# A third extra seven-product unit in each half of a SwiGLU down product: units (9, 13, 19) and (5, 9, 13) instead of (9, 19) and (5, 13)

## The chip, the cores and the metric

The kernel runs on one core of a Trainium2 chip. The metric is the device time of one execution in microseconds (us), the median of several runs. The engines that matter here are TensorE (PE, matmuls), its weight loader (PEld), VectorE (DVE), ScalarE (ACT) and SyncE (SP), which issues the loads of weights. Each of them takes its instructions in the order of its own queue, and an instruction that waits holds up all that stand behind it.

## What is computed

One decoder layer on 256 tokens of width 2048: a SwiGLU feed-forward block (FFN), a mixer of two gated linear attentions, and a second FFN, each with a norm before and a norm after it. The change lies in the last matrix product of both FFNs, `hidden @ w_down`, with a hidden width of 5504.

```python
def swiglu(x, w_gate, w_up, w_down):
    return (jax.nn.silu(x @ w_gate) * (x @ w_up)) @ w_down

f1 = swiglu(rms_norm(h, ffn1_pre_norm[l]), ffn1_w_gate[l], ffn1_w_up[l], ffn1_w_down[l])
h = h + 0.5 * rms_norm(f1, ffn1_post_norm[l])
...
f2 = swiglu(rms_norm(h, ffn2_pre_norm[l]), ffn2_w_gate[l], ffn2_w_up[l], ffn2_w_down[l])
h = h + 0.5 * rms_norm(f2, ffn2_post_norm[l])
```

## The kernel before

All products are exact to float32 by splitting each operand into a high and a low part: ACT writes the high part (`whi`, L151), DVE the rest (`wlo`, L153), and `mm3` (L155 to L159) makes one product of a 128x128 block of activations and a 128x512 block of weights by three matmuls: high x high (L157), low activations x high weights (L158), high activations x low weights (L159).

`down_proj` (L587) makes the down product in two halves of 1024 output columns. A half has two column blocks of 512 (`i` = 0, 1), there are two blocks of 128 tokens (`t` = 0, 1), and the hidden width is cut into 43 k tiles of 128. The four sums of a half, c00, c01, c10 and c11, stay in PSUM. Two k tiles make a unit: units 0 to 20, and one single k tile (42). A plain unit takes 2 x 2 x 2 = 8 products, that is 24 matmuls, and its weights are two chunks of 128x1024, each split by one ACT and one DVE instruction.

A unit of the list `DSUMS + DMORE[hf]` is done by Strassen's scheme in the form of Winograd (`Blocks.seven`, L265): seven products, that is 21 matmuls, but sums of weight blocks have to be made first. DVE makes three adds (`wsum`, `raw`, `wsum`, L243), then the three low parts: two of 128x1024 (`wlo`, L243) and one of 128x1536 (`wsuml`, L243). ACT makes four high parts (L278, L280, L282, L284), and SP issues four loads of 256 KB (L272 to L275) where a plain unit has two of 512 KB. The seven products go to four shared sums (p1, p5, p6, p7) and three of the c; `share` (L304) and `close` (L317) add the p to the c at the end of the half.

A seven unit also needs sums of activation blocks. `sums_of(u)` (L756) makes them one unit ahead: four small DVE operations (L203 to L206), then ACT (high) and DVE (low). They are kept in `parts`, which both halves share, so a unit that is in both halves is summed once. Where they are kept differs: units 3, 7, 11 and 15 have homes of their own, and the units of `DMORE` take buffers from `new_part`:

```python
def new_part(i):
    s = ("hkhi", "hklo")[i]
    return fwork.tile([P, 2, NT * P], F32R, tag=s, name=nm(s), bufs=4)
```

There are four buffers of `hkhi` and four of `hklo`. The same buffers take the split activations of every unit (`get`, L739, through L151 and L153): one `hkhi` and one `hklo` for each unit, 22 times in each half. A buffer is free again when the last matmul that reads it is done. So sums of activations that lie in them take from the buffers in which the units' own activations are prepared ahead of PE. Before, unit 9's sums are held only until unit 9 of the first half is done, 19's likewise, and 5's and 13's in the second half.

The weights have rings of five buffers (`raw`, `whi`, `wlo`), so ACT and DVE can be about five chunks ahead of PE. The order of instructions on each engine is fixed when the program is built: a scheduler takes the instructions in the order of the code, and where a buffer is not free it lets other work of that engine go first. `weigh` (L600) squares a finished c on ACT (L452) and multiplies it with the post norm on DVE (L608).

Of the kernel before, what the change touches and what calls it, by code (L numbers as in the profile page):

```python
# [31 lines left out]
SUMS = (2, 4, 6)  # L32
FOUR = (2, 4, 5, 6)
DSUMS = (3, 7, 11, 15)
DMORE = ((9, 19), (5, 13))
DTAIL = 7
O_GQ, O_GK, O_GV, O_GO, O_CODE = 0, 512, 1024, 2048, 3072
O_HQ, O_HF, O_HI, O_HO, O_ZG, O_ZH = 3088, 4112, 5136, 6160, 7184, 9232
# [48 lines left out]
def kernel(ctx: ExitStack, tc: tile.TileContext, a: dict, out: bass.AP):  # L87
# [499 lines left out]
    def down_proj(w_dram, nkt, lhs, sums_of, post, pre, wpost, ys, homes, following):  # L587
# [30 lines left out]
        for hf in range(2):  # L618
# [4 lines left out]
            n = nkt - DTAIL if hf else nkt  # L623
            units = sorted(DSUMS + DMORE[hf])
            kt = 0
# [49 lines left out]
    def ffn(pre, x, rs, post, pre_next, begin=None, ready=(), then=None):  # L675
        with ExitStack() as fctx:
# [4 lines left out]
# [3 lines that stand above are left out]
# [72 lines left out]
            def sums_of(u):  # L756
# [3 lines left out]
                          *[f[:, k * P:(k + 1) * P] for k in range(4)])  # L760
                if any(u in more for more in DMORE):
                    hi, lo = [new_part(i).rearrange("p i c -> p (i c)") for i in range(2)]
# [600 lines left out]
```

## Time and profile before

| | |
|---|---|
| median of 3 runs | 2080.27 us (2080.07 to 2080.61) |
| the profiled execution | 2080.67 us |
| its span, first to last instruction | 2078.8 us |
| PE busy | 2067.8 us |
| DVE busy | 1854.7 us |
| ACT busy | 1239.7 us |
| down product of the first FFN | from about 466 to 692 us of the span |
| down product of the second FFN | from about 1844 to 2070 us |

Times in rows of the timeline are microseconds from the start of the span, then the duration, engine, line, operation, output, inputs and form. Where a row has brackets, they give the idle time of the engine before it and what ended it. Instructions overlap: an engine's next instruction can start before the one ahead has ended, so the step from start to start is what an engine needs for one. Of a matmul the end is modelled.

### The profile page before, as it was taken

The page shows a single profiled execution, that of the slowest core. Times are in us where ns is not written, and L with a number is a line of the kernel's source. Part 1 is how long each engine was busy: PE and PEld are TensorE (multiplying, and loading weights), DVE is VectorE, ACT ScalarE, POOL GpSimd, SP SyncE. Part 2 cuts the span into 40 slices and gives each one's busy share as a digit, 9 for nine tenths or more (in the row PEclk, how much of TensorE's full clock was granted, in tenths as well). Part 3 has the DMA queues.
Part 4 walks back from the last instruction along what each step waited for, and adds up shares of the span by engine and source line. Part 5 has one row for each costly group of instructions (what it writes and reads, how often), then busy time and mean ns, then how long its engine had stood idle before and what let it go on. Part 6 is the DMA issues. An engine that isn't in the chain of part 4 may idle for free.

```text
span 2078.8 us, 29319 instructions
## 1 busy us (share of the span) xinstructions
PE 2067.8 (99%) x10509; PEld 1721.1 (83%) x10509; DVE 1854.7 (89%) x2187; ACT 1239.7 (60%) x1670; POOL 40.6 (2%) x87
## 2 busy tenths in 40 slices
PE   9999999999999999999999999999999999999998
PEld 7888888898888888878888888888888888898886
DVE  7898999989999879989999897578999989999896
ACT  6555656565666576576655554465555655666663
POOL 1000000000000100000000000010000000000000
PEclk9999999999999999999999999999999999999999
DMA  8566656656667467555565666755666657576663
GB/s 267 183 210 199 211 188 194 214 183 226 208 195 233 153 192 232 163 168 188 174 203 186 184 221 214 220 179 172 222 200 186 209 186 224 165 239 201 198 208 132
DMA packets 200665, 412.23 MB, mean 198 GB/s; under 512 B 18036, under 2 KB 26423, under 8 KB 200520
## 3 DMA queue, kind: packets, MB, share of 16 engines
q1 hardware_dynamic: 194896, 401.80, 61.0%
q10 hardware_dynamic: 5624, 8.57, 1.3%
q8 instruction: 82, 1.34, 0.3%
q14 instruction: 63, 0.52, 0.1%
HBM read 406.11 MB, written 4.19 MB: 197 GB/s over the span
## 4 chain that ended last, share of the span: by engine, by line
PE 96%; ACT 1%; DVE 1%; issue 0%; DMA 0%; POOL 0%; SPq 0%; DVEq 0%; POOLq 0%; ACTq 0%
PE c L157 22%; PE c L159 21%; PE c L158 21%; PE p L159 5%; PE p L158 5%; PE p L157 5%; PE mm L157 3%; PE mm L159 3%; PE mm L158 3%; PE ps L397 2%; PE acc L157 1%; PE acc L158 1%; PE acc L159 1%; PE ps L905 0%; DVE h L510 0%
## 5 line engine op out<-in xcount | busy, mean ns | idle before, releaser
L151 ACT ACTIVATE whi<-raw 128x1024 fp32r<-128x1024 f32 (+3 forms) x498 | 510.6, 1033 | 279.8 <-PE c L158 114.7
L153 DVE TENSOR_TENSOR wlo<-raw,whi 128x1024 fp32r<-128x1024 f32 (+3 forms) x498 | 587.5, 1190 | 86.6 <-ACT whi L151 85.3
L157 PE MATMUL c<-whi,xhi 128*128 128x512 f32 (+1 forms) x1270 | 495.8, 391 | 0.5 <-DVE hq L849 0.3
L159 PE MATMUL c<-wlo,xhi 128*128 128x512 f32 (+1 forms) x1270 | 490.8, 387 | 0.0
L158 PE MATMUL c<-whi,xlo 128*128 128x512 f32 (+1 forms) x1270 | 490.5, 386 | 0.0
L243 DVE TENSOR_TENSOR wlo<-raw,whi 128x1024 fp32r<-128x1024 f32 (+1 forms) x252 | 294.5, 1203 | 11.9 <-ACT whi L278 6.3
L159 PEld LDWEIGHTS c<-wlo,xhi 128*128 128x128 f32 x1270 | 238.4, 188 | 47.2 <-DVE wlo L153 0.3
L157 PEld LDWEIGHTS c<-whi,xhi 128*128 128x128 f32 x1270 | 238.5, 188 | 46.9 <-issue 0.7
L158 PEld LDWEIGHTS c<-whi,xlo 128*128 128x128 f32 x1270 | 238.6, 188 | 44.9
L282 ACT ACTIVATE whi<-raw 128x1024 fp32r<-128x1024 f32 (+1 forms) x126 | 131.8, 1046 | 204.5 <-DVE raw L243 78.5
L243 DVE TENSOR_TENSOR wsuml<-wsum,wsumh 128x1536 fp32r<-128x1536 f32 (+1 forms) x126 | 218.0, 1730 | 33.7 <-ACT wsumh L284 33.6
L157 PE MATMUL c<-whi,hkhi 128*128 128x512 f32 x558 | 217.0, 389 | 0.0
L159 PE MATMUL c<-wlo,hkhi 128*128 128x512 f32 x558 | 216.8, 388 | 0.0
L158 PE MATMUL c<-whi,hklo 128*128 128x512 f32 x558 | 216.7, 388 | 0.0
L280 ACT ACTIVATE wsumh<-wsum 128x1024 fp32r<-128x1024 f32 (+1 forms) x126 | 131.5, 1044 | 108.6 <-DVE wsum L243 74.7
L278 ACT ACTIVATE whi<-raw 128x1024 fp32r<-128x1024 f32 (+1 forms) x126 | 131.4, 1043 | 100.2 <-PE c L158 84.7
L243 DVE TENSOR_TENSOR wsum<-raw,raw 128x1024 f32<-128x1024 f32 (+1 forms) x126 | 151.8, 1205 | 20.5 <-DMA raw<-in_ffn_w_down_dram 17.3
L159 PEld LDWEIGHTS c<-wlo,hkhi 128*128 128x128 f32 x558 | 104.8, 188 | 21.6
L158 PEld LDWEIGHTS c<-whi,hklo 128*128 128x128 f32 x558 | 104.8, 188 | 21.3
L157 PEld LDWEIGHTS c<-whi,hkhi 128*128 128x128 f32 x558 | 104.8, 188 | 21.3
L243 DVE TENSOR_TENSOR c<-c,psum 128x512 f32<-128x512 f32 (+1 forms) x135 | 86.6, 682 | 11.8 <-PE c L159 11.4
L243 DVE TENSOR_TENSOR wsum<-raw 128x512 f32<-128x512 f32 (+1 forms) x126 | 86.0, 683 | 3.6
(347 smaller groups left out, 3117.1 us busy)
## 6 DMA issues: line engine op xcount, KB each, us to landing
raw<-in_ffn_w_down_dram SPq DMA_DIRECT2D x124, 512.0 KB, 4.6
raw<-in_w_in_dram SPq DMA_DIRECT2D x104, 512.0 KB, 4.5
raw<-in_ffn_w_up_dram SPq DMA_DIRECT2D x97, 512.0 KB, 4.5
raw<-in_ffn_w_gate_dram SPq DMA_DIRECT2D x96, 512.0 KB, 4.7
raw<-in_ffn_w_gate_dram SPq DMA_DIRECT2D x128, 256.0 KB, 3.8
raw<-in_w_in_dram SPq DMA_DIRECT2D x128, 256.0 KB, 3.5
raw<-in_ffn_w_up_dram SPq DMA_DIRECT2D x126, 256.0 KB, 3.8
raw<-in_ffn_w_down_dram SPq DMA_DIRECT2D x96, 256.0 KB, 4.0
```

The lines of the kernel that those rows point to most:

```text
L151: last[0] = nc.scalar.activation(hi, src, AF.Copy)
L153: nc.vector.tensor_tensor(lo, src, hi.bitcast(F32), op=ALU.subtract)
L157: nc.tensor.matmul(ps, lhsT=xhi, rhs=whi, start=start, stop=False)
L158: nc.tensor.matmul(ps, lhsT=xlo, rhs=whi, start=False, stop=False)
L159: nc.tensor.matmul(ps, lhsT=xhi, rhs=wlo, start=False, stop=stop)
L243: return nc.vector.tensor_tensor(o, x, y, op=op)
L278: nc.scalar.activation(ahi, ra, AF.Copy)
L280: nc.scalar.activation(hi[:, 0:2, :], wsum[:, 0:2, :], AF.Copy)
L282: nc.scalar.activation(bhi, rb, AF.Copy)
L397: end = nc.tensor.transpose(dst_ps[:, i * P:(i + 1) * P], src[:, i * P:(i + 1) * P], ident)
```

## The change

One table is changed: which units beside 3, 7, 11 and 15 are done with seven products, in the first and in the second half of the down product. It holds for both FFNs.

```diff
-DMORE = ((9, 19), (5, 13))
+DMORE = ((9, 13, 19), (5, 9, 13))
```

Unit 13 of the first half and unit 9 of the second become seven units. Units 9 and 13 are now in both halves, so their sums are made in the first half and held until the second half has used them. PE has 12 matmuls fewer, DVE 16 instructions more, ACT 8 more, and SP issues 16 loads of 256 KB in place of 8 of 512 KB. The order of the work changes at three places, the same in both FFNs; the numbers below are of the first FFN.

The first place is DVE at the step from unit 11 to unit 12 of the first half. Before, `hklo_996` is the low part of unit 12's activations, and `wlo_994` and `wlo_999` are the low parts of unit 12's weights:

```order
L243 TENSOR_TENSOR wlo_987_4679<-raw_981_4669,whi_986_4678 128x1024
L153 TENSOR_TENSOR hklo_996_4724<-hT_563_2734,hkhi_995_4723 128x512
L243 TENSOR_TENSOR wlo_989_4681<-raw_982_4670,whi_988_4680 128x1024
L243 TENSOR_TENSOR wsuml_985_4673<-wsum_983_4671,wsumh_984_4672 128x1536
L153 TENSOR_TENSOR wlo_994_4720<-raw_992_4717,whi_993_4719 128x1024
L153 TENSOR_TENSOR wlo_999_4742<-raw_997_4739,whi_998_4741 128x1024
```

Now, at the same place on DVE, `sums_992` and `hklo_994` are the sums of unit 13, `wlo_997` and `wlo_1002` the weights of unit 12, and `hklo_999` is unit 12's activations:

```order
L243 TENSOR_TENSOR wsuml_985_4673<-wsum_983_4671,wsumh_984_4672 128x1536
L153 TENSOR_TENSOR wlo_997_4729<-raw_995_4726,whi_996_4728 128x1024
L203 TENSOR_TENSOR sums_992_4717<-hT_563_2734 128x128
L205 TENSOR_TENSOR sums_992_4717<-hT_563_2734 128x128
L204 SCALAR_TENSOR_TENSOR sums_992_4717<-sums_992_4717,hT_563_2734 128x128
L153 TENSOR_TENSOR wlo_1002_4751<-raw_1000_4748,whi_1001_4750 128x1024
L206 TENSOR_TENSOR sums_992_4717<-hT_563_2734,sums_992_4717 128x128
L153 TENSOR_TENSOR hklo_994_4723<-sums_992_4717,hkhi_993_4722 128x512
L153 TENSOR_TENSOR hklo_999_4733<-hT_563_2734,hkhi_998_4732 128x512
L243 TENSOR_TENSOR wsum_1005_4768<-raw_1003_4766,raw_1004_4767 128x1024
```

Unit 12's activations have moved from ahead of unit 11's last two low parts to behind unit 13's sums, and ACT's high part of them likewise.

The second place is the end of the first half. The rows are DVE before: `hklo_1102` is the activations of unit 0 of the second half, `psum` the shared sums, c00 to c11 the finished sums of the first half, and `y` their product with the post norm:

```order
L243 TENSOR_TENSOR psum_1074_5083<-psum_1074_5083,p7_909_4318 128x512
L153 TENSOR_TENSOR hklo_1102_5176<-hT_106_590,hkhi_1101_5175 128x512
L243 TENSOR_TENSOR psum_1075_5084<-psum_1074_5083,p5_908_4317 128x1024
L153 TENSOR_TENSOR hklo_1107_5210<-hT_106_590,hkhi_1106_5209 128x512
L153 TENSOR_TENSOR wlo_1105_5206<-raw_1103_5203,whi_1104_5205 128x1024
L243 TENSOR_TENSOR c00_865_4150<-c00_865_4150,psum_1074_5083 128x512
```

Now on DVE `hklo_1108` is the activations of that unit 0:

```order
L243 TENSOR_TENSOR c00_865_4150<-c00_865_4150,psum_1080_5100 128x512
L243 TENSOR_TENSOR c01_866_4151<-c01_866_4151,psum_1081_5101 128x512
L243 TENSOR_TENSOR c10_867_4152<-c10_867_4152,psum_1080_5100 128x512
L608 TENSOR_TENSOR y_1096_5171<-c00_865_4150,held_862_4147 128x512
L243 TENSOR_TENSOR c11_868_4153<-c11_868_4153,psum_1081_5101 128x512
L608 TENSOR_TENSOR y_1098_5176<-c01_866_4151,held_862_4147 128x512
L153 TENSOR_TENSOR hklo_1108_5193<-hT_106_590,hkhi_1107_5192 128x512
```

The activations of the next half's first unit have moved behind the four closing adds and two of the products with the post norm. A little earlier, on PE, units 18, 19 and 20 were done one after the other, and now they are mixed. These rows are PE now, at the end of unit 18 (`hkhi_1058`); `hkhi_1053` is the sums of unit 19, `hkhi_1072` the activations of unit 19 and `hkhi_1082` those of unit 20:

```order
L159 MATMUL c11_868_4153<-wlo_1062_5025,hkhi_1058_5006 128x512
L157 MATMUL c01_866_4151<-whi_1068_5049,hkhi_1053_4996 128x512
L158 MATMUL c01_866_4151<-whi_1068_5049,hklo_1054_4997 128x512
L159 MATMUL c01_866_4151<-wlo_1069_5050,hkhi_1053_4996 128x512
L159 MATMUL p7_909_4318<-wsuml_1067_5044,hkhi_1053_4996 128x512
L157 MATMUL p1_906_4315<-whi_1068_5049,hkhi_1072_5063 128x512
L157 MATMUL c00_865_4150<-whi_1070_5051,hkhi_1072_5063 128x512
L157 MATMUL c10_867_4152<-wsumh_1066_5043,hkhi_1072_5063 128x512
L157 MATMUL c01_866_4151<-whi_1075_5090,hkhi_1082_5106 128x512
```

With the sums of 9, 13 and 19 held, one buffer is left for the units' own activations, and unit 19's can be written only when unit 18's are read for the last time. PE has four products of unit 19 that need only sums there; seven more of these matmuls stand ahead of unit 18.

The third place is ACT at the step from unit 3 to unit 4 of the second half. Before, `hkhi_1135` is the sums of unit 5, `hkhi_1140` the activations of unit 4, `hkhi_1154` those of unit 5, `whi_1150` and `whi_1152` the weights of unit 5:

```order
L278 ACTIVATE whi_1150_5393<-raw_1145_5384 128x1024
L151 ACTIVATE hkhi_1135_5340<-sums_1134_5335 128x512
L151 ACTIVATE hkhi_1140_5350<-hT_261_1314 128x512
L151 ACTIVATE hkhi_1154_5407<-hT_261_1314 128x512
L280 ACTIVATE wsumh_1148_5387<-wsum_1147_5386 128x1024
L282 ACTIVATE whi_1152_5395<-raw_1146_5385 128x1024
```

Now, on ACT, `hkhi_1141` is the sums of unit 5, `hkhi_1146` the activations of unit 4, and `whi_1156` and `whi_1158` the weights of unit 5:

```order
L278 ACTIVATE whi_1156_5410<-raw_1151_5401 128x1024
L151 ACTIVATE hkhi_1141_5357<-sums_1140_5352 128x512
L282 ACTIVATE whi_1158_5412<-raw_1152_5402 128x1024
L151 ACTIVATE hkhi_1146_5367<-hT_261_1314 128x512
L280 ACTIVATE wsumh_1154_5404<-wsum_1153_5403 128x1024
L284 ACTIVATE wsumh_1154_5404<-wsum_1153_5403 128x512
```

The activations of unit 4 now stand behind a high part of unit 5's weights (L282), which is made of a block that DVE has summed. With the sums of 9, 13 and 5 held, they take the buffer of unit 3's activations, after the last matmul of unit 3.

## The prediction

> **What bounds the kernel now.** I read the page first (its busy times and the chain of work), then a table of windows over the two down products, then the timelines of PE, DVE and ACT at the places where the order of the work changes.
>
> ```profile
> span 2078.8 us, 29319 instructions
> PE 2067.8 (99%) x10509; PEld 1721.1 (83%) x10509; DVE 1854.7 (89%) x2187; ACT 1239.7 (60%) x1670; POOL 40.6 (2%) x87
> PE 96%; ACT 1%; DVE 1%; issue 0%; DMA 0%; POOL 0%; SPq 0%; DVEq 0%; POOLq 0%; ACTq 0%
> ...
> 440.00:680.00 240.00, 240.00 (x1098) 203.07 (x1097) 222.06 (x268) 153.47 (x197) 0.52 (x3) 1.00 0.68 217
> 1840.00:2050.00 210.00, 210.00 (x936) 174.58 (x935) 193.76 (x233) 133.61 (x168) 0.50 (x2) 1.00 0.65 208
> 2050.00:2078.00 28.00, 20.27 (x90) 16.46 (x88) 12.85 (x20) 3.20 (x9) 2.12 (x7) 0.93 0.20 75
> ```
>
> The chain is PE's. In both down products (the first two windows; after the length stand PE, PEld, DVE, ACT and POOL) PE never stops and DVE is busy for 93% and 92%. So a matmul removed is worth its step on PE, and any new wait of PE is paid in full.
>
> ```profile
> 528.51 0.39 PE L158 MATMUL c<-wsumh,hklo 128*128 128x512 f32 x1
> ...
> L157 PE MATMUL c<-whi,hkhi 128*128 128x512 f32 x558 | 217.0, 389 | 0.0
> ...
> 528.74 0.39 PE L159 MATMUL c<-wsuml,hkhi 128*128 128x512 f32 x1
> 528.97 0.39 PE L157 MATMUL c<-whi,hkhi 128*128 128x512 f32 x1
> 529.19 0.39 PE L158 MATMUL c<-whi,hklo 128*128 128x512 f32 x1
> ```
>
> **What is removed.** One more seven unit in each of two halves of two FFNs: 4 x 3 = 12 matmuls. Each takes a step of 0.227 us (528.74, 528.97, 529.19), not the mean duration of 389 ns, because they overlap. Gain: 12 x 0.227 = **2.7 us**. [...]
>
> What is added beside PE: each new seven unit gives DVE 6.4 us in place of 2.3 us (steps below), ACT two instructions more, SP two more loads. The average leaves room for it: 8.3 us in 240 us, where DVE is idle for 18. The loads carry the same bytes at a DMA share of 0.68 and are ahead of DVE at the places below; I cost them at nothing. The sums are made once per FFN as before, only earlier. What costs time is the order: the sums of 9 and 13 now hold two of the four buffers of activations from the first half into the second, and other work is pushed past.
>
> For the hand-offs I use these rows.
>
> ```profile
> 576.11 0.39 PE L158 MATMUL c<-whi,hklo 128*128 128x512 f32 x1
> ...
> 576.54 1.06 ACT L151 ACTIVATE whi<-raw 128x1024 fp32r<-128x1024 f32 x1 [1.66 <-PE c L158]
> 577.50 0.61 ACT L151 ACTIVATE hkhi<-hT 128x512 fp32r<-128x512 f32 x1
> ...
> 676.95 0.42 DVE L153 TENSOR_TENSOR hklo<-hT,hkhi 128x256 fp32r<-128x256 f32 x1
> ...
> 677.43 0.49 PE L158 MATMUL c<-held,hklo 128*128 128x512 f32 x1
> 677.76 0.40 PE L159 MATMUL c<-held,hkhi 128*128 128x512 f32 x1
> ```
>
> A matmul's start lets ACT start 0.43 us later (576.11 to 576.54). ACT's step for 1024 columns is 0.96. DVE's end at 677.37 lets PE go at 677.43, and the next matmul comes 0.33 instead of 0.23 later: 0.16 us in all from an operand's end to PE.
>
> **Place 1, unit 12 of the first half.**
>
> ```profile
> 522.97 0.68 DVE L153 TENSOR_TENSOR hklo<-hT,hkhi 128x512 fp32r<-128x512 f32 x1
> 523.58 1.22 DVE L243 TENSOR_TENSOR wlo<-raw,whi 128x1024 fp32r<-128x1024 f32 x1
> 524.71 1.75 DVE L243 TENSOR_TENSOR wsuml<-wsum,wsumh 128x1536 fp32r<-128x1536 f32 x1
> 526.38 3.49 DVE L153 TENSOR_TENSOR wlo<-raw,whi 128x1024 fp32r<-128x1024 f32 x3
> ...
> 531.52 0.28 DVE L203 TENSOR_TENSOR sums<-hT 128x128 f32<-128x128 f32 x1
> 531.73 0.28 DVE L205 TENSOR_TENSOR sums<-hT 128x128 f32<-128x128 f32 x1
> ...
> 533.26 0.28 DVE L206 TENSOR_TENSOR sums<-hT,sums 128x128 f32<-128x128 f32 x1
> ...
> 533.58 0.63 ACT L151 ACTIVATE sums<-sums 128x512 fp32r<-128x512 f32 x1 [2.47 <-DVE sums L206]
> ```
>
> DVE's steps are 0.61 (hklo), 1.13 (wlo), 1.67 (wsuml) and 0.2 (a small sum). So a plain unit's low parts take 2.3, and a seven's 3 x 1.13 + 2 x 0.67 + 1.67 = 6.4, with 0.67 for the dependent adds of 512 columns (estimate from hklo's step). The hklo at 522.97 is unit 12's; now it comes later, so wsuml starts at 524.1, the first wlo at 525.8, three small sums at 526.9, the second wlo at 527.5, and the last sum ends at 528.9. ACT makes its high part 0.04 later (533.54 to 533.58) in 0.63, then unit 12's own, until 530.1; DVE makes the sums' low part and then unit 12's, until 530.9. PE wants these at 528.97 and 529.19. It is late by 530.93 + 0.16 - 529.19 = **1.9 us**. If DVE had the low part first, 1.3 would be left (the high part); if it is half a step later, 2.5.
>
> ```profile
> 1898.52 0.68 DVE L153 TENSOR_TENSOR hklo<-hT,hkhi 128x512 fp32r<-128x512 f32 x1
> ...
> 1907.14 0.39 PE L158 MATMUL c<-whi,hklo 128*128 128x512 f32 x1
> ```
>
> In the second FFN the same hklo starts 8.6 us ahead of PE's need, not 6.2 (522.97 to 529.19), so by the same sum it is ready 0.5 us in time: 0, at most 0.6.
>
> **Place 2a, units 17 to 20 of the first half.** PE takes seven matmuls of unit 19 ahead of unit 18, so unit 19's weights are wanted a unit earlier. From unit 12's activations to the second low part of unit 19's weights DVE has 17 steps of 1024 columns, 13 of 512, two wsuml and eight small sums: 17 x 1.13 + 13 x 0.61 + 2 x 1.67 + 8 x 0.2, with 0.3 for dependent adds, 32.4 us. PE comes to it 140 matmuls after unit 12's start: 140 x 0.227 = 31.7. With the hand-off PE waits some 0.9 us in the first FFN, and 0.4 in the second, which is 0.5 ahead (bounds 0 and 1.5). After unit 18 only four matmuls need no activations: 0.9 us of cover. ACT first makes a high part of weights (start 0.43 after the matmul ahead of the last, then 0.96), then unit 19's (0.62). Counted from the last matmul's start that is 0.2 + 0.96 + 0.62 + 0.16 = 1.95 against 4 x 0.227 + 0.23 = 1.13: 0.8 late, and 0.2 more for the low part, **1.0 us** in each FFN (bounds 0.6 and 1.5).
>
> **Place 2b, the step into the second half.**
>
> ```profile
> 578.83 0.39 PE L158 MATMUL c<-whi,hklo 128*128 128x512 f32 x1
> ...
> 579.28 0.39 PE L157 MATMUL c<-whi,hkhi 128*128 128x512 f32 x1
> ...
> 580.19 0.39 PE L158 MATMUL c<-whi,hklo 128*128 128x512 f32 x1
> ...
> 579.31 1.06 ACT L151 ACTIVATE whi<-raw 128x1024 fp32r<-128x1024 f32 x1 [0.44 <-ACT sq L452]
> 580.27 0.62 ACT L151 ACTIVATE hkhi<-hT 128x512 fp32r<-128x512 f32 x1
> 580.79 0.58 ACT L452 ACTIVATE sq<-c 128x512 bf16<-128x512 f32 x1
> 581.27 0.19 ACT L452 ACTIVATION_READ_ACCUMULATOR sq<-c 128x1 f32 x1
> ```
>
> The first half's last tile starts at 576.57 in these coordinates. Its eleventh matmul (578.83) frees a weight buffer; ACT's high part starts 0.43 later, at 579.26, and now the square of c01 stands behind it: 580.22 to 580.9 (0.67 with its accumulator read, 580.79 to 581.46). DVE's product with the post norm waits for that square, and the new half's first hklo is behind it in the queue: 580.93 + 0.61 = 581.54, ready at 582.2, on PE at 582.4. PE, which takes four L157 ahead, wants it at 580.19: **2.2 us** late in each FFN. In the trace this hklo was made about 6 us ahead. Bounds: 1.5 (the square ahead of the weights) and 2.9.
>
> **Place 3, unit 4 of the second half.**
>
> ```profile
> 595.61 0.39 PE L157 MATMUL p<-whi,hkhi 128*128 128x512 f32 x1
> ...
> 595.63 1.06 ACT L278 ACTIVATE whi<-raw 128x1024 fp32r<-128x1024 f32 x1 [1.71 <-PE c L158]
> ...
> 597.24 0.69 DVE L153 TENSOR_TENSOR hklo<-sums,hkhi 128x512 fp32r<-128x512 f32 x1 [0.79 <-ACT hkhi L151]
> ...
> 600.37 0.39 PE L157 MATMUL c<-whi,hkhi 128*128 128x512 f32 x1
> ```
>
> DVE is held by ACT until 597.24; then wsum at 597.85 and raw at 599.0, ready at 599.7. ACT makes the high part of that block (1.05, until 600.8), and behind it unit 4's activations (until 601.3). PE wants the block at 600.37 and has it at 600.95: 0.6 late; two matmuls on, the activations are 0.1 late. Two later hand-offs of the same buffer, for units 5 and 6, cost 0.1 each by the same steps. **0.9 us** in each FFN (bounds 0.3 and 1.8).
>
> **The sum.** Waits: 1.9 + (0.9 + 0.4) + 2 x 1.0 + 2 x 2.2 + 2 x 0.9 = 11.4 us. Less 2.7: +8.7 us, which on the profiled execution's 2080.67 (span 2078.8 and 1.9 around it) is 2089.4. The median is 0.4 lower than that execution, so I forecast **2089.0 us** (2080.27 + 8.7), 0.4% slower. With all low bounds (1.3 + 0 + 1.2 + 3.0 + 0.6 = 6.1) it is 2083.7, with all high ones (3.1 + 3.0 + 3.0 + 5.8 + 3.6 = 18.5) 2096.1; both at once are unlikely.
>
> **Rivals.** *The cover holds* (no wait is seen): -2.7 us, 2077.6 us, 0.13% faster than before, and less than the 0.2% that can be told from no change. For it speaks DVE's idle 18 us in 240 and low parts that are often several us ahead of PE. Against it: what is late is ordered late, not for lack of capacity. It decides if unit 0's hklo of the second half ends by 580.0 in the coordinates above. Chance 0.07. *One place pays*: only 2b: -2.7 + 4.4 = +1.7, 2082.0; only 3: 2079.4. It needs ACT to be quicker than its rows. Chance 0.08. *The clock drops*: in the window from 2050 PE is idle for 7.7 of 28 us and the granted clock is 0.93, so 0.07 x 28 = 2.0 us of matmul time are lost there. If each of the four groups of waits costs as much, it adds 8: 2097. Against it: the groups hold 2 to 5 us of idle, in pieces. Chance 0.05. [...] That the change isn't made is excluded: the order has 12 matmuls fewer.
>
> **Chances and range.** The forecast has 0.80. Slower by over 0.2% (about what a measurement can tell) is above 2084.4: 0.85 from the forecast and the clock. Within 0.2%: 0.14, from the other two. Faster: 0.01, as only 2.7 us are there to gain. The range of 2083.5 to 2095.0 leaves out the three rivals.
>
> **What would show it.** PE's instructions 10497, DVE's 2203, ACT's 1678. PE idle grows from 11 us by about 11, in gaps at these places: matmuls of c waiting for `hklo` L153 near 580 (over 2 us) and 529 (only in the first FFN), for `hkhi` L151 after units 18 of the first and 3 of the second half. If PE shows no gap near 580 and 1958, the largest term falls; if it shows waits for `wlo` through units 13 to 15, DVE is short of capacity, which I cost at nothing there.

## The result, and the profile after

| | before | changed |
|---|---|---|
| median | 2080.20 us (6 runs, 2079.99 to 2081.21) | 2096.31 us (6 runs, 2092.81 to 2098.37) |
| ratio | | 1.0074, 95% interval 1.0061 to 1.0087 |
| profiled execution | 2080.67 us | 2098.37 us |

The change makes the kernel 16.1 us slower where 8.7 were forecast, and 1.3 us outside the range. The page of the changed kernel, its span and busy times:

```profile
span 2096.6 us, 29366 instructions
PE 2074.7 (99%) x10497; PEld 1720.2 (82%) x10497; DVE 1872.0 (89%) x2203; ACT 1245.2 (59%) x1678; POOL 40.4 (2%) x87
```

PE has its 12 matmuls less, and yet 6.9 us more of busy time (2067.8 before): not only waits were added, matmuls have become slower. The view of PE's waits (what it waited for, us in total, times, longest) has five rows that belong to the down products. Before, PE waited for none of these; all its rows were

```profile
PE ps L1303 <- POOL idle L1298: 1.3, 1, 1.3
PE ps L965 <- ACT state L975: 0.4, 1, 0.4
PE c L157 <- DVE hq L849: 0.3, 1, 0.3
PE ps L1307 <- DMA ident<-in_c_ident_dram: 0.2, 1, 0.2
```

and the five rows now:

```profile
PE c L158 <- DVE hklo L153: 4.1, 3, 1.9
PE p L159 <- DVE wlo L243: 2.1, 2, 1.0
PE p L157 <- ACT whi L282: 2.0, 4, 0.6
PE c L157 <- ACT hkhi L151: 1.3, 1, 1.3
PE p L157 <- ACT hkhi L151: 1.2, 2, 0.6
```

PE's timeline at the start of the second half in the first FFN:

```profile
583.87 1.07 PE L157 MATMUL c<-whi,hkhi 128*128 128x512 f32 x4
586.85 0.50 PE L158 MATMUL c<-whi,hklo 128*128 128x512 f32 x1 [1.91 <-DVE hklo L153]
587.18 0.39 PE L159 MATMUL c<-wlo,hkhi 128*128 128x512 f32 x1
...
588.15 0.63 PE L159 MATMUL c<-wlo,hkhi 128*128 128x512 f32 x1
588.58 0.63 PE L158 MATMUL c<-whi,hklo 128*128 128x512 f32 x1
...
591.52 0.40 PE L159 MATMUL c<-wlo,hkhi 128*128 128x512 f32 x1
591.76 0.39 PE L157 MATMUL c<-whi,hkhi 128*128 128x512 f32 x1
```

The wait is where it was forecast. Counted by steps, from the fourth L157's start at 584.55 to 586.85 and on to 587.18, it costs 2.30 + 0.33 - 2 x 0.227 = 2.2 us. What follows was given 1 chance in 20: from 588.15 on a matmul takes 0.43 in place of 0.227 us, until 591.5. The table of windows, cut at these moments (length, PE's busy time, its instructions, granted clock, DMA):

```profile
584.63:588.04 3.41, 1.50 (x7) 1.00 0.34 123
588.04:591.46 3.42, 3.42 (x10) 0.50 0.20 40
591.46:594.87 3.41, 3.41 (x16) 1.00 0.69 240
1946.55:1949.96 3.41, 1.79 (x7) 1.00 0.65 210
1949.96:1953.38 3.42, 3.42 (x9) 0.50 0.85 275
1970.44:1973.86 3.42, 1.51 (x8) 1.00 0.38 137
1973.86:1977.27 3.41, 3.41 (x10) 0.50 0.00 0
```

Three times a stretch of 3.41 us in which PE did little is followed by one of the same length at half clock. Each costs 3.41 x (1 - 0.227 / 0.43) = 1.6 us. Summed by places, each step of PE above 0.227 us counted:

| place | forecast, FFN 1 and 2 | measured, FFN 1 and 2 |
|---|---|---|
| 1: unit 12 of the first half | 1.9, 0 | 2.2, 0.3 |
| 2a: unit 19's first product | 0.9, 0.4 | 1.9, 2.1 |
| 2a: after unit 18 | 1.0, 1.0 | 1.0, 1.0 |
| 2b: start of the second half | 2.2, 2.2 | 2.2, 2.2 |
| 3: units 4 to 6 of the second half | 0.9, 0.9 | 1.2, 1.2 |
| half-clock stretches | 0 | 3 x 1.6 |
| 12 matmuls | -2.7 | -2.7 |
| sum | +8.7 | +17.4 (spans: +17.8) |

### The profile page after: what moved, and what is told of

It is laid out like the page before. It is cut to its first block, busy times and chain, and to the rows that moved or that the text cites. A ratio compares the mean times of both kernels' runs of the same rounds, so it can differ in the third digit from the quotient of the medians.

```text
span 2096.6 us, 29366 instructions
## 1 busy us (share of the span) xinstructions
PE 2074.7 (99%) x10497; PEld 1720.2 (82%) x10497; DVE 1872.0 (89%) x2203; ACT 1245.2 (59%) x1678; POOL 40.4 (2%) x87
## 5 line engine op out<-in xcount | busy, mean ns | idle before, releaser
L151 ACT ACTIVATE whi<-raw 128x1024 fp32r<-128x1024 f32 (+3 forms) x490 | 502.0, 1033 | 275.5 <-PE c L158 120.5
L153 DVE TENSOR_TENSOR wlo<-raw,whi 128x1024 fp32r<-128x1024 f32 (+3 forms) x490 | 578.3, 1190 | 91.5 <-ACT whi L151 90.5
L157 PE MATMUL c<-whi,xhi 128*128 128x512 f32 (+1 forms) x1270 | 496.0, 391 | 0.4 <-ACT xhi L469 0.2
L243 DVE TENSOR_TENSOR wlo<-raw,whi 128x1024 fp32r<-128x1024 f32 (+1 forms) x260 | 303.7, 1204 | 11.9 <-ACT whi L278 6.3
L157 PEld LDWEIGHTS c<-whi,xhi 128*128 128x128 f32 x1270 | 238.4, 188 | 47.0 <-ACT xhi L469 0.6
L282 ACT ACTIVATE whi<-raw 128x1024 fp32r<-128x1024 f32 (+1 forms) x130 | 136.2, 1048 | 232.2 <-DVE raw L243 87.8
L243 DVE TENSOR_TENSOR wsuml<-wsum,wsumh 128x1536 fp32r<-128x1536 f32 (+1 forms) x130 | 225.1, 1732 | 33.6 <-ACT wsumh L284 33.4
L158 PE MATMUL c<-whi,hklo 128*128 128x512 f32 x534 | 209.4, 392 | 4.2 <-DVE hklo L153 4.1
L159 PE MATMUL c<-wlo,hkhi 128*128 128x512 f32 x534 | 209.2, 392 | 0.0
L157 PE MATMUL c<-whi,hkhi 128*128 128x512 f32 x534 | 205.3, 393 | 1.3 <-ACT hkhi L151 1.3
L278 ACT ACTIVATE whi<-raw 128x1024 fp32r<-128x1024 f32 (+1 forms) x130 | 135.8, 1044 | 117.0 <-PE c L158 99.6
L243 DVE TENSOR_TENSOR wsum<-raw,raw 128x1024 f32<-128x1024 f32 (+1 forms) x130 | 156.7, 1205 | 10.8 <-DMA raw<-in_ffn_w_down_dram 6.5
L157 PEld LDWEIGHTS c<-whi,hkhi 128*128 128x128 f32 x534 | 101.0, 190 | 23.1 <-ACT hkhi L151 2.7
```

The costliest lines, as they stand in the source:

```text
L151: last[0] = nc.scalar.activation(hi, src, AF.Copy)
L153: nc.vector.tensor_tensor(lo, src, hi.bitcast(F32), op=ALU.subtract)
L157: nc.tensor.matmul(ps, lhsT=xhi, rhs=whi, start=start, stop=False)
L158: nc.tensor.matmul(ps, lhsT=xlo, rhs=whi, start=False, stop=False)
L159: nc.tensor.matmul(ps, lhsT=xhi, rhs=wlo, start=False, stop=stop)
L243: return nc.vector.tensor_tensor(o, x, y, op=op)
```

## The experiments

Medians in us; the ratio is to the kernel before, run on the same chip.

| run | median | ratio and 95% interval |
|---|---|---|
| e1: sums of 9 and 13 in homes of their own | 2080.85 | 1.0002 (0.9993 to 1.0010) |
| e2: sums held, no unit more | 2093.35 | 1.0058 (1.0046 to 1.0071) |
| e3, e18: five buffers | 2077.97, 2077.94 | 0.9989 (0.9980 to 0.9998), 0.9989 (0.9980 to 0.9997) |
| e12: before, with five buffers | 2079.95 | 0.9999 (0.9990 to 1.0008) |
| e5: unit 13 alone added | 2080.93 | 1.0006 (0.9997 to 1.0015) |
| e6: unit 9 alone added | 2080.12 | 0.9998 (0.9989 to 1.0007) |
| e7: no unit in both halves | 2093.82 | 1.0065 (1.0052 to 1.0077) |
| e8: sums made twice | 2083.36 | 1.0018 (1.0009 to 1.0027) |
| e4, e10: changed, matmuls of zeros in a wait | 2093.78, 2095.46 | 1.0066 (1.0053 to 1.0078), 1.0074 (1.0061 to 1.0086) |
| e9: changed, again | 2095.32 | 1.0070 (1.0056 to 1.0084) |
| e11, e13: only 9 at home | 2080.70, 2080.53 | 1.0004 (0.9996 to 1.0013), 1.0002 (0.9993 to 1.0011) |
| e14: e13 with matmuls of zeros | 2084.64 | 1.0020 (1.0010 to 1.0029) |
| e15: e13 with later loads | 2079.74 | 0.9997 (0.9988 to 1.0006) |
| e16: changed, with later loads | 2097.20 | 1.0076 (1.0063 to 1.0090) |
| e17: e1 with later loads | 2078.85 | 0.9993 (0.9984 to 1.0002) |

**Is it the held sums, or DVE's work?** Homes: the part of `home` that units 3 and 7 leave unused.

```diff
-                if any(u in more for more in DMORE):
+                if u in (9, 13):
+                    home = homes_of[0 if u == 9 else 1]
+                    hi, lo = home[:, 2, :], home[:, 3, :]
+                elif any(u in more for more in DMORE):
```

> The changed kernel, but the sums of units 9 and 13 lie in the unused halves of the homes of units 3 and 7; the four buffers of hkhi and hklo serve as before the change. Held-buffer theory: all waits of the five places go (PE idle back to about 11 us in the profile), no half-clock stretch inside the down products, and only the 12 matmuls' gain is left: 2080.2 - 2.7 = 2077.5 us. Rival (the seven units' own work on DVE and ACT is what PE waits for): the waits stay, 2089 us or more.

Holding alone: the table is `((9, 19), (9, 13))`, and one line sums unit 13 in the first half, where nothing uses it.

```diff
+                if not hf and kt == 24 and 13 not in parts:
+                    parts[13] = sums_of(13)
```

> No seven unit more than before (9, 19 in the first half, 9, 13 in the second: 10509 PE instructions), but the sums of 9 and 13 are both made in the first half and held into the second, as in the changed kernel. Held-buffer theory: waits at the end of the first half and at the start of the second, 4 to 6 us in each FFN, with up to two half-clock stretches of 1.7 us: 2088 to 2095 us. Rival (DVE's work): as many seven units as before, so 2080 us, within 1 us.

Five buffers: `bufs=4` becomes `bufs=5` in `new_part`, in the changed kernel and in the kernel before.

> The changed kernel with five buffers of hkhi and of hklo in place of four. Held-buffer theory: two buffers are left where there was one, the order of PE is changed at one short place only, and nearly all waits go: 2077.5 to 2081 us. Rival (DVE's work): 2089 us or more.

> The kernel before with five buffers of hkhi and hklo. PE waits nowhere in its down products, so a fifth buffer has nothing to give: 2080.2 us, within 0.5. If the fifth buffer alone brought the gain of the run with five buffers, it would be 2078 here too; if DVE's preparing further ahead makes low parts late, 2081 to 2083.

Waits of PE in e2, where no unit is added (the rows of its down products):

```profile
PE c L158 <- DVE hklo L153: 4.5, 3, 1.9
PE p L157 <- ACT hkhi L151: 1.5, 2, 0.8
PE c L157 <- ACT hkhi L151: 1.4, 1, 1.4
```

Holding alone brings places 1, the second of 2a, and 2b, and 13 us. Unit 19's first product waits for nothing that counts there (the view has no row for its `whi` or `wlo`), though PE takes it ahead of unit 18 as in the changed kernel. What differs up to there is that unit 13 is a plain unit in that half, which gives DVE less to do. With five buffers all seven units are there, DVE has the same 2203 instructions, and the whole list of PE's waits is the three of the kernel's start and the mixer:

```profile
PE ps L1303 <- POOL idle L1298: 1.3, 1, 1.3
PE ps L965 <- ACT state L975: 0.4, 1, 0.4
PE ps L1307 <- DMA ident<-in_c_ident_dram: 0.2, 1, 0.2
```

So the loss belongs to the buffers, not to the seven units. The fifth buffer gives the kernel before nothing (e12), and e3 and e18 have a good part of the 2.7 us: 2.5 and 2.2. The spans of their profiled executions, 2076.2 and 2076.1 against 2078.8, are 2.6 and 2.7 shorter. The homes gave no gain, against the expectation; that is taken up below.

**One sum or two?** The table with one of the units only: `((9, 13, 19), (5, 13))` and `((9, 19), (5, 9, 13))`.

> Unit 13 in both halves, unit 9 in the first only: ((9, 13, 19), (5, 13)); 6 matmuls fewer than before, one held sum. Theory that only the second held sum is too much (two buffers left beside the passing sums are enough, one is not): 2080.3 - 1.4 = 2079 us, at most one wait under 1 us for each FFN. Rival (each held sum costs its half): 2080.3 + 8 = 2088 us.

> Unit 9 in both halves, unit 13 in the second only: ((9, 19), (5, 9, 13)); 6 matmuls fewer than before, one held sum. As for the unit 13 alone: 2079 us if only the second held sum is too much, 2088 us if each held sum costs its half.

Neither has a wait at places 2a, 2b or 3, so only the second held sum is too much there. Unit 13 alone has place 1, a wait of 1.6 for `hkhi` and 0.3 for `hklo`, which takes more than its six matmuls give and is more than the one microsecond that was allowed for. Unit 9 alone has no such wait; its span is 1.2 us shorter (2077.6 against 2078.8), but the medians don't show it.

**Ways round the holding.** Other units, `((9, 17, 19), (1, 5, 13))`, and sums that are given up at the half (`parts.pop(u, None)` for the first half's units) and made again:

> As many seven units as in the changed kernel (10497 PE instructions), but none of the table in both halves: ((9, 17, 19), (1, 5, 13)), so no sums are held from half to half. Held-buffer theory: no waits from holding; the order of PE is changed around units 19 and 20 and the start of the second half, where seven units now lie close (17, 19, then 1, 3, 5), so 2077.5 us and up to 6 us of waits there: 2078 to 2084. Rival (two more seven units are too much for DVE wherever they are): 2089 or more.

> The changed kernel, but the sums of 9, 13 and 19 are given up at the end of the first half, and those of 9 and 13 made again in the second: DVE has 20 small steps more, 4 us in all, and no sum is held across. Held-buffer theory: waits at the ends of the halves go; DVE is short of a few us around units 11 to 15 as with the sums in homes of their own: 2078 to 2082 us. Rival (DVE's work decides): slower than the changed kernel, 2097 or more.

Choosing units that are in one half only is no cure, and e7 is 10 us slower than was expected: it waits 3.0 us in each FFN for unit 4's activations of the second half, which stand behind the sums of unit 5, and the mean granted clock of its profiled execution is 0.997 (0.999 for the kernel before). Three seven units follow closely there (1, 3, 5), and DVE falls behind (its row has no gap from 598 to 608 us). That is the time that the rival foretold, but not its reason: e3 has as many seven units and no wait. Making the sums twice takes most of it away. What is left, 1.4 us more than was expected, is place 1 with 2.4 us, smaller waits (0.7 us for `hkhi` and 0.9 for `hklo` in all), and a mean granted clock of 0.998 in the profiled execution, where the kernel before has 0.999.

**The clock.** Eight matmuls of a zero block at place 2b, and the changed kernel again:

```diff
+                    for _ in range(8):
+                        nc.tensor.matmul(b.c[0][0], lhsT=zeros, rhs=chunk[0][0],
+                                         start=False, stop=False)
```

> The changed kernel with eight matmuls of a zero block (added to c00, which they leave as it is) where PE waits for the low activations at the start of the second half: 16 matmuls more. Clock theory (PE idle for about half of a stretch of 3.4 us is followed by 3.4 us of steps of 0.43 in place of 0.227 us, which costs 1.7 us): no half-clock stretch behind that place in either FFN; the changed kernel's profile has two there, so the median falls by 1 to 3.5 us, to 2093 to 2095 us, with a smaller spread. Rival (only the wait itself costs, and the slow steps have another cause): 2096 us, or 2097 if the eight matmuls outlast the wait.

> The changed kernel once more, as it is, beside the next three on one chip. By the windows of the profiles so far (a stretch of 3.413 us of a grid that runs on its own is followed by one at half clock when PE is idle for over 1.4 to 1.6 us of it), its time without any half-clock stretch is 2092.6 us, and each adds 1.7: runs near 2092.7, 2094.4, 2096.1 and 2097.8, with the same waits within 0.1 us in the profile. If the slow steps belong to the code, the profile has them behind the same three waits as the first time, and the runs don't spread.

> The eight matmuls of zeros at the start of each second half again, now on the same chip as the changed kernel: median 1 to 3 us under it by the clock theory, as the two waits of 1.9 us bring no half-clock stretch any more; the same or 0.3 us more if only the wait costs.

The windows of e9, which is the changed kernel once more:

```profile
528.01:531.43 3.42, 1.38 (x6) 1.00 0.68 202
531.43:534.84 3.41, 3.41 (x9) 0.50 0.29 110
586.04:589.45 3.41, 1.90 (x8) 1.00 0.16 56
589.45:592.86 3.41, 3.41 (x16) 1.00 0.40 80
1968.44:1971.85 3.41, 1.50 (x7) 1.00 0.24 82
1971.85:1975.26 3.41, 3.41 (x9) 0.50 0.16 18
```

This time place 1 is followed by half clock, which it was not the first time (from 526.60 the first profile has 2.58 us of PE's time in 3.42, and 1.00 behind it), and place 2b of the first FFN is not, with the same wait of 1.9 us. In the trace of the first profile the half-clock stretches begin at 588.04, 1949.96 and 1973.86 us and take 3.413 us each, and the distances between their starts are 399.0 and 7.0 of that length. In e9, 1971.85 - 531.43 is 422.0 of it. The borders at 586.04 and 589.45 are put there by the same step, 16 and 17 of it behind 531.43, which is an estimate: the stretch between them then holds 1.51 us of idle, and 0.4 of the wait lies ahead of it. So where the slow stretches lie against the code differs between the two executions.

In the windows taken, a stretch has a granted clock of 0.50 behind it with 1.19 us of PE's time in it (e4, from 1946.70), with 1.38 and 1.50 (e9), and with 1.50, 1.51 and 1.79 (the changed kernel's first profile). It has 1.00 behind it with 1.64 (e13, from 527.90), 1.82 (e5, from 527.66), 1.90 (e9) and 1.92, 2.00 and 2.05 (e16). By this modelled time the two overlap, 1.79 and 1.64. By the matmuls that start in them, cut by the same step, they touch: 5, 6 and 6 in the three of the first profile; 6, too, in the last stretch of its second down product, from 2086.50, which 1.00 follows; 9 or more in all its others at 1.00 there. What decides between them is not shown.

The waits of e9 were not all the same, as had been expected. Its rows of the down products are

```profile
PE c L158 <- DVE hklo L153: 4.1, 3, 1.9
PE c L157 <- ACT hkhi L151: 2.5, 2, 1.7
PE p L159 <- DVE wlo L243: 1.8, 2, 1.0
...
PE p L157 <- ACT hkhi L151: 1.2, 2, 0.6
PE p L157 <- ACT whi L282: 1.2, 2, 0.6
```

The matmuls of c wait twice for `hkhi`, 2.5 us, where the first profile has one of 1.3, and L282 holds PE up twice in place of four times. The sum holds nevertheless: 10.8 us in these rows, where the first profile's five have 10.7 and cost 15.3 with the hand-offs. By that measure (an estimate) 15.4 us of waits and two half-clock stretches less 2.7 make 2096.1 us, and this execution took 2095.77.

With the waits filled, e4 has no half clock at place 2b:

```profile
584.78:588.20 3.42, 3.37 (x15) 1.00 0.28 98
588.20:591.61 3.41, 3.41 (x16) 1.00 0.20 32
```

Nor does 0.50 follow at that place in e4's second FFN (from 1970.60, 3.35 us of PE's time in 3.40). In e10 PE's waits for `hklo` are 0.3 us in all (4.1 in e9). But the median of e10 is not under that of e9 (2095.46 and 2095.32), against the expectation. In both runs with zeros, unit 19 of the second FFN waits 1.4 us, where the changed kernel waits 0.6 in one profile and not at all in the other; in e4 half clock follows there (from 1950.12), as it does in the first of these two. The second FFN's order of work up to that place is the same in all four; why PE waits longer in e4 and e10 is not shown. A second trial has one single wait, at place 1:

> The kernel with unit 9's sums at home and 13's in the ring once more, as the measure for the next two: 2080.7 us, with one wait of 2.4 us at unit 12 of the first FFN, in some executions followed by a half-clock stretch (runs near 2080.4 and near 2082.2).

> As the run before, with nine matmuls of zeros ahead of unit 12 of the first FFN, 2.0 us of work where PE waits 2.4. Clock theory: the wait for operands ends as late as before, but the stretch is never idle for over 1.6 us, so no half-clock stretch follows in any execution: the runs near 2082 to 2084 go, all lie within 2079.8 to 2081.2, and the profile shows 1.00 behind unit 12. If slow steps have another cause, runs spread to 2084 as before.

Nine matmuls of zeros ahead of unit 12 took the place of most of the wait, and no slow step follows (from 532.34 on PE's steps are 0.23 us). But on DVE and ACT the order of the work behind unit 12 is now another, unit 18 waits 1.3 us, and the median rose by 4.1 where it was to stay. The profiled execution rose by 1.9; the rest is not explained. PE's timeline of e14:

```profile
529.08 2.26 PE L644 MATMUL c<-whi,zeros 128*128 128x512 f32 x9
531.18 0.50 PE L159 MATMUL c<-whi,hkhi 128*128 128x512 f32 x1
...
564.86 0.50 PE L160 MATMUL c<-whi,hklo 128*128 128x512 f32 x1 [1.28 <-DVE hklo L155]
```

So with the waits at place 2b filled the granted clock behind them stayed at 1.00 (e4, both FFNs), but as a cure filling is not shown.

**Place 1: the number of buffers, or late blocks?** Only unit 9's sums at home leave three buffers for the passing work, as five less two do.

> Only the sums of unit 9 in the unused half of unit 3's home; those of 13 in the ring, which leaves three buffers for the passing work from unit 12 on, as five buffers less two do. If only the number of buffers that are left counts: the same as with five buffers, 2078 us, and no wait for wlo in units 13 and 15 (with both sums at home, four are left, DVE prepares activations further ahead and the low parts of weights come late there, 3 us). Rival (a sum in a home of its own costs those waits by itself): 2080 us, with a wait for wlo in unit 13.

The expectation failed: the buffers left are as many as in e3, and the order of DVE at unit 12 is the same row by row, but PE waits 2.4 us. DVE does those rows 3.2 us later, and it lost 2.1 of them at unit 7, where it stood 3.55 us for the blocks that it sums and 1.46 in e3. Around that moment ACT's queue issues the four loads of the post norm's weights. They were moved:

```diff
-                if not hf and kt in (8, 9, 10, 11):
-                    load_bcast(wpost[kt - 8], post, kt - 8, last[0])
+                if not hf and kt in (32, 33, 34, 35):
+                    load_bcast(wpost[kt - 32], post, kt - 32, last[0])
```

> As the run before last, but the four loads of the post norm's weights (256 KB each, on ACT's queue) are issued at k tiles 32 to 35 of the first half in place of 8 to 11. Load theory of place 1: DVE stands for unit 7's blocks because these loads share the DMA engines with them; without them it stands under 1.5 us in place of 3.55, stays 2 us further ahead, and PE's wait at unit 12 falls from 2.7 to under 1 us: 2078 to 2079 us. Rival (DVE falls behind through the sums of unit 13 alone, or the blocks are late for want of a free buffer): the wait stays over 2 us, 2080.7.

DVE's timeline of e13, and of e15, at unit 7 (in brackets the idle time and its end):

```profile
494.33 1.23 DVE L243 TENSOR_TENSOR wsum<-raw,raw 128x1024 f32<-128x1024 f32 x1 [3.68 <-DMA raw<-in_ffn_w_down_dram]
```

```profile
492.01 1.23 DVE L243 TENSOR_TENSOR wsum<-raw,raw 128x1024 f32<-128x1024 f32 x1 [1.40 <-DMA raw<-in_ffn_w_down_dram]
```

The blocks land sooner, as the DMA view of both from 484 to 494 us has it (KB each, us from issue to landing), first e13, then e15:

```profile
raw<-in_ffn_w_down_dram SPq DMA_DIRECT2D x4, 256.0 KB, 7.6
```

```profile
raw<-in_ffn_w_down_dram SPq DMA_DIRECT2D x4, 256.0 KB, 5.2
```

PE's wait at unit 12 falls from 1.8 and 0.3 to this one row of e15:

```profile
PE c L158 <- DVE hklo L153: 0.2, 1, 0.2
```

The spans of the two profiled executions differ by 2.2 us (2079.4 and 2077.2). The median falls by 0.8 us only (2080.53 to 2079.74), less than expected and less than the intervals resolve. With five buffers the blocks land in 5.8 us (e3, the median of six such loads from 478 to 496 us; 7.6 of four in e11) and DVE stands 1.46 us there without that edit, and e3 has no place 1; why they land sooner with a fifth buffer is not shown. The same edit on e1 and on the changed kernel:

> Both sums in homes of their own and the post norm's loads at k tiles 32 to 35. If the late blocks of unit 7 are also what made the low parts of units 13 and 15 late there (3 us), DVE stands under 1.5 us for them and those waits go: 2077.5 to 2079 us. Rival (with four buffers left DVE prepares activations too far ahead): the waits for wlo stay, 2080.8 us.

> Five buffers again, on the same chip as the run before: 2078 us, no wait of PE in the down products. If both versions are free of waits they agree within 0.5 us.

> The changed kernel with the same four loads at k tiles 32 to 35. Place 1 in the first FFN falls as in the run before (by 2 us if the load theory holds); the other places stay, or unit 19's blocks come later still, since the loads are now just ahead of units 17 to 19: 2092 to 2096 us.

In both, DVE stands less at unit 7: 1.47 us in e17 and 3.21 in e1, 1.45 in e16 and 2.73 in the changed kernel. In e17 the waits for `wlo` go from 2.2 to 0.6 us, so the same late blocks had made e1 miss its 2077.5; what is left is about what e17 lies above e18. In e16 the wait of matmuls of c for `hkhi`, place 1 in the changed kernel, is down to 0.4 us from 1.3; at place 2b (two waits of 1.9 us for `hklo`) and after unit 18 (two of 0.6 for `hkhi`) nothing changes. The longest wait for `whi` L282 is now 1.1 us, where the changed kernel has 0.6; why is not shown. The granted clock behind its waits at units 19 and 2b is 1.00 (windows from 565.11, 585.59 and 1967.98), 0.999 is on record for that execution, and it took 2091.8 us, where the other four took 2096.6 to 2098.0 at 0.995 to 0.997.

## Why the prediction was wrong in size

**Right.** The 12 matmuls are worth 2.7 us: with no wait left, e3 and e18 are 2.2 to 2.5 us under before by their medians and 2.6 to 2.7 by their spans. The order, not the amount, of the work is what costs: "what is late is ordered late, not for lack of capacity". Places 2b (2.2 in each FFN) and after unit 18 (1.0) came out to the tenth, place 1 within 0.3, place 3 within 0.3. The rival that the cover holds fell.

Of the profiled execution's 17.4 us, 8.7 were not forecast: 4.8 for the clock, 2.7 at place 2a, 0.6 each at places 1 and 3.

**Wrong: the clock.** "The clock drops" had a chance of 0.05, with the reason that "the groups hold 2 to 5 us of idle, in pieces". Pieces did not keep it out: 5, 6 and 6 matmuls start in the three stretches ahead of the slow ones, and a wait of 1.9 us with its slow hand-off had half clock behind it in three of the four cases at place 2b (both FFNs of the changed kernel's first profile, the second of e9). That its price, 2.0 us, came near the measured 1.6 is luck: the slow stretch of the kernel before, from which it was read, begins at 2074.15 us (granted clock 0.50 from there on), and the last matmul starts at 2069.88. Luck, too, is that its 2097 lies near the median, since it has four drops on top of waits that were put too low. By the sum of the measured waits an execution without it takes 2080.2 - 2.7 + 15.3 = 2092.8 us, and the fastest of 11 took 2092.74; the slowest, 2098.37, has three. The median lies 3.5 higher, about two stretches. The granted clock on record for the six runs goes with it: 0.999 at 2092.81, 0.998 at 2093.47 and 2095.10, 0.997 at 2097.51 and above.

**Wrong: place 2a.** Unit 19's first product was put at 0.9 and 0.4 us and took 1.9 and 2.1. The failed sentence is that on the loads: "I cost them at nothing". The sum counted DVE's steps only, and the blocks were not "ahead of DVE". ACT's timeline of the changed kernel in the second FFN:

```profile
1937.81 1.06 ACT L151 ACTIVATE whi<-raw 128x1024 fp32r<-128x1024 f32 x1 [1.53 <-DMA raw<-in_ffn_w_down_dram]
1938.77 0.61 ACT L151 ACTIVATE hkhi<-hT 128x512 fp32r<-128x512 f32 x1
...
1943.70 1.06 ACT L278 ACTIVATE whi<-raw 128x1024 fp32r<-128x1024 f32 x1 [2.75 <-DMA raw<-in_ffn_w_down_dram]
...
1946.90 1.06 ACT L282 ACTIVATE whi<-raw 128x1024 fp32r<-128x1024 f32 x1 [0.28 <-DVE raw L243]
```

DVE's:

```profile
1939.42 0.69 DVE L153 TENSOR_TENSOR hklo<-hT,hkhi 128x512 fp32r<-128x512 f32 x1 [1.13 <-ACT hkhi L151]
...
1943.11 1.22 DVE L153 TENSOR_TENSOR wlo<-raw,whi 128x1024 fp32r<-128x1024 f32 x1
1944.30 1.23 DVE L243 TENSOR_TENSOR wsum<-raw,raw 128x1024 f32<-128x1024 f32 x1
...
1947.37 2.35 DVE L243 TENSOR_TENSOR wlo<-raw,whi 128x1024 fp32r<-128x1024 f32 x2
```

and PE's:

```profile
1948.01 0.50 PE L157 MATMUL p<-whi,hkhi 128*128 128x512 f32 x1 [0.58 <-ACT whi L282]
...
1949.78 0.66 PE L159 MATMUL p<-wlo,hkhi 128*128 128x512 f32 x1 [1.04 <-DVE wlo L243]
```

ACT stands 1.53 us for a block of unit 18, and the high part of unit 17's activations is behind it (1938.77). So DVE, which makes their low part, loses 1.13 us, its only gap from unit 12's activations on. In the first FFN it loses 0.89 in the same place. After that its row is unbroken up to the low parts of unit 19 at 1947.37. Unit 19's own blocks, for which ACT stands 2.75 us, hold DVE up by less than 0.1 us (from 1943.11 to 1944.30 it steps 1.19 in place of 1.13). The forecast's 0.9 (0.8, as 140 x 0.227 is 31.8) and the lost 0.89 come near the first FFN's 1.9. In the second, 0.4 and 1.13 leave half a microsecond, and there DVE came to unit 12 0.3 us late, where it was forecast to be 0.5 ahead. With unit 18 ahead, as in e3, where the high part of L282 is done at 560.97 (559.91 and 1.06), PE has no wait at unit 19, and a loss of 1 us does not show.

**Also missed:** that place 1 does not belong to the held buffers alone. It needs unit 13's sums in the first half (e5 has it, e6 not) and DVE late from unit 7's blocks (e15). That e2 costs 13 us with no unit added, and e1 and e3 none of the waits at 2a, 2b and 3 with all of them, leaves the held buffers as the cause of the rest.

**Open.** What a filled wait is worth could not be measured, since other waits came with the filler. Of the 2.7 us, the medians of e3 and e18 lack 0.2 to 0.5, which intervals of 1.9 us either way don't resolve. Why the blocks of units 17 to 19 land when they do, and why unit 19's waits differ in e9, is not shown.

## What to carry to other kernels

A value that is kept across a stage in a ring takes a buffer from the work ahead for all that time: count what is left at the tightest moment. Here two buffers beside the passing sums cost little and one cost 15 us of waits, for the sake of 2.7. And where PE is the bound, read the granted clock behind a wait as well as its length: here a wait of 1.9 us at place 2b had 3.41 us at 0.50 behind it in three of four cases, which cost 1.6 us more, and 11 executions of the same program took 2092.74 to 2098.37 us, so a gain is compared over many executions.

## What was not expected of the hardware

A granted clock of 0.50 inside a down product, behind stretches in which PE did little but still worked: 3.41 us of it at a time, three times in the changed kernel's first profile (1.50, 1.51 and 1.79 us of PE's time in the stretch ahead) and in two of three windows of e9 (1.38 and 1.50). Behind 1.64 in e13 and 1.90 in e9 it was 1.00.

With four loads of 256 KB on ACT's queue the blocks of a seven unit landed in 7.6 us, without them in 5.2 (e13 and e15), and the wait that went with it showed 35 us after DVE's, at unit 12 (494.33 and the stretch from 527.90 in e13). This is with four buffers: with five, 5.8 us was seen with the loads in their old place (e3).
